# Four sums of weight blocks per pair of gate and up units, formed by accumulating SBUF-to-SBUF transfers from GpSimd instead of by VectorE

## The chip, the cores and the metric

The kernel runs on 1 core of one Trainium2 chip. The metric is the device time of one execution in microseconds (us). Before the change it is 2313.14 us, the median of 3 runs (2313.03 to 2313.42).

## The reference

Two layers of an encoder, for 64 + 512 tokens (columns) of width 1024 that share all weights. Each layer has a feed-forward network (FFN), a mixer and a second FFN, so the kernel runs four FFNs in all:

```
x = x + 0.5 * rmsnorm(swiglu(rmsnorm(x)))      # FFN 1
x = x + rmsnorm(mix(rmsnorm(x)) @ w_out)       # mixer: attention, recurrence, chunk MLP
x = x + 0.5 * rmsnorm(swiglu(rmsnorm(x)))      # FFN 2

def _swiglu(x, w_gate, w_up, w_down):
    return (jax.nn.silu(x @ w_gate) * (x @ w_up)) @ w_down
```

w_gate and w_up are 1024 x 2816, that is 8 x 22 blocks of 128 x 128, in fp32. Only their products with x are touched here.

## The kernel before

A product in fp32 is made of three products of halves: `split` writes a high part (ScalarE, line 138) and the rest, the low part (VectorE, line 139), and `three` issues high*high, high*low and low*high on TensorE (line 68). A weight block of 128 x 1024 (512 KB: four 128-row blocks of gate, four of up) so costs one load (two DMA issues of 256 KB on SP, line 454), one ScalarE pass into a tile wh and one VectorE pass into a tile wl.

The first two of the 22 units of each FFN are multiplied plainly (tiles u). The other twenty go in ten pairs f, f+1 through `seven`, which saves one product in eight: the eight products of a 2 x 2 scheme (two halves of the inner dimension, two units; two halves of the 576 columns on the other side) become seven, of sums of weight blocks with sums of activations. `combine` forms the sums of activations once for each FFN (tiles b, th, tl; lines 427 to 442), just before the first pair. The sums of weights are formed for each pair. With a11, a12 the lower and upper half of unit f's rows and a21, a22 those of unit f+1, the parts are

```
p1 = a11                   p5 = s = a21 + a22
p6 = s + a11               p3 = s + a11 + a12
p7 = a21 + a11             p2 = a12         p4 = a22
```

and TensorE takes them in the order p1, p5, p6, p3, p7, p2, p4, with results in X (p1, p6, p7, p4), Q (p5, p3) and R (p2). s grows in place: each step adds one block after the split of the step before. The four sums of a pair stand at lines 478 (s = a21 + a22), 480 (a21 += a11), 488 (s += a11) and 497 (s += a12), all on VectorE.

Raw blocks live in a pool of six buffers (tile names wr, and ws for s), split blocks in seven pairs of buffers, one for each part. A pair holds five raw buffers, so a buffer passes to the next pair when its block has been read for the last time. The order of instructions on each engine is fixed when the program is built, by a scheduler; every engine and every DMA queue then takes its instructions in that order. SP issues all DMAs, GpSimd does a few small operations of the norms (lines 151 and 198) and of the mixer.

Of the kernel before, what the change touches and what calls it, by code (L numbers as in the profile page):

```python
# [8 lines left out]
F32 = mybir.dt.float32  # L9
# [3 lines left out]
ALU = mybir.AluOpType  # L13
AX = mybir.AxisListType

P = 128
# [33 lines left out]
class Net:  # L50
# [396 lines left out]
    def seven(self, f, wg, wu, ops, g, rbc):  # L447
        nc = self.nc

        def load(k0, c):  # L450
            raw = self.wraw.tile([P, 1024], F32, name=self.name("wr"), tag="wr")
            for e, w in enumerate((wg, wu)):
                src = w.rearrange("(k p) f -> p k f", p=P)[:, k0:k0 + 4, c * P:(c + 1) * P]
                nc.sync.dma_start(raw[:, e * 512:(e + 1) * 512].rearrange("p (k n) -> p k n", k=4), src)
            return raw

        def part(raw):
            hi = self.whi.tile([P, 1024], F32R, name=self.name("wh"), tag="wh")
            lo = self.wlo.tile([P, 1024], F32R, name=self.name("wl"), tag="wl")
            self.split(hi, lo, raw)  # L460
            return hi, lo


        def product(w, b, ps, start):
            for e in range(2):
                for k in range(4):
                    c = e * 512 + k * P
                    h = ops[b][k // 2]
                    s = slice((k % 2) * W2, (k % 2 + 1) * W2)
                    self.three(ps[e][:, :W2], w[0][:, c:c + P], w[1][:, c:c + P], h[0][:, s], h[1][:, s],  # L470
                               start and k == 0, k == 3, not start)
                    self.tick()

        A, B = slice(0, W2), slice(W2, T)
        a11, a21, a22 = load(0, f), load(0, f + 1), load(4, f + 1)
        p1 = part(a11)
        s = self.wraw.tile([P, 1024], F32, name=self.name("ws"), tag="wr")
        nc.vector.tensor_tensor(s, a21, a22, op=ALU.add)
        p5 = part(s)
        nc.vector.tensor_tensor(a21, a21, a11, op=ALU.add)  # L480
        a12 = load(4, f)
        X = [self.mm("X"), self.mm("X")]
        product(p1, "b11", X, True)
        p1 = None
        s1 = [self.slot("s1"), self.slot("s1")]
        for e in range(2):
            nc.scalar.activation(s1[e][:, A], X[e][:, :W2], AF.Copy)
        nc.vector.tensor_tensor(s, s, a11, op=ALU.add)
        a11 = None
        p6 = part(s)  # L490
        Q = [self.mm("Q"), self.mm("Q")]
        product(p5, "t1", Q, True)
        p5 = None
        s5 = self.slot("s5")
        for e, h in enumerate((A, B)):
            nc.scalar.activation(s5[:, h], Q[e][:, :W2], AF.Copy)
        nc.vector.tensor_tensor(s, s, a12, op=ALU.add)  # L497
        p3 = part(s)
        s = None
        product(p6, "t2", X, False)  # L500
        p6 = None
        for e in range(2):
            nc.scalar.activation(s1[e][:, B], X[e][:, :W2], AF.Copy)
        p7 = part(a21)
        a21 = None
        product(p3, "b22", Q, False)
        p3 = None
        g[f] = self.slot("g")
        t = [g[f], s1[1]]
        for e in range(2):  # L510
            nc.vector.tensor_tensor(t[e][:, B], s1[e][:, B], Q[e][:, :W2], op=ALU.add)
        Q = None
        p2 = part(a12)
        a12 = None
        product(p7, "t3", X, False)
        p7 = None
        for e, h in enumerate((A, B)):
            nc.vector.tensor_tensor(s5[:, h], s5[:, h], X[e][:, :W2], op=ALU.add)
        g[f + 1] = self.slot("g")
        nc.vector.scalar_tensor_tensor(g[f + 1][:, B], s5[:, A], -1.0, rbc[:, B], op0=ALU.mult, op1=ALU.mult)  # L520
        p4 = part(a22)
        a22 = None
        R = [self.mm("R"), self.mm("R")]
        product(p2, "b21", R, True)
        p2 = None
        for e in range(2):
            nc.vector.tensor_tensor(t[e][:, A], s1[e][:, A], R[e][:, :W2], op=ALU.add)
        R = None
        nc.vector.tensor_tensor(t[0], t[0], rbc, op=ALU.mult)
        nc.scalar.activation(t[0], t[0], AF.Silu)  # L530
        nc.vector.tensor_tensor(g[f], t[0], t[1], op=ALU.mult)
        s1 = t = None
        product(p4, "t4", X, False)
        p4 = None
        u = g[f + 1]
        nc.vector.scalar_tensor_tensor(u[:, A], X[0][:, :W2], -1.0, rbc[:, A], op0=ALU.mult, op1=ALU.mult)
        nc.scalar.activation(u, u, AF.Silu)
        nc.vector.scalar_tensor_tensor(u[:, B], s5[:, B], -1.0, u[:, B], op0=ALU.mult, op1=ALU.mult)
        nc.vector.scalar_tensor_tensor(u[:, A], X[1][:, :W2], -1.0, u[:, A], op0=ALU.mult, op1=ALU.mult)
# [917 lines left out]
```

## Time and profile before

| | |
|---|---|
| median of 3 runs | 2313.14 us |
| the profiled execution | 2313.43 us, of which the span is 2311.6 us |
| TensorE (PE) busy | 2217.3 us, 96% |
| VectorE (DVE) busy | 1594.7 us, 69% |
| ScalarE (ACT) busy | 1114.0 us, 48% |
| GpSimd (POOL) busy | 225.4 us, 10% |
| DMA queue of SP | 208.54 MB, 30.3% of 16 engines |
| the ten pairs of the first FFN | 60.07 to 278.67 us of the span |

Busy time is summed over the span. The chain of waits follows the work that ended last back from the end, at each step to what released it. PEclk is the granted share of TensorE's clock. The pairs of the four FFNs take some 220 us each; the rest of an FFN is its first two units, the sums of activations and the down projection.

### The profile page before, as it was taken

What the parts mean: (1) busy time and instruction counts of PE and PEld (TensorE: products, weight loads), DVE (VectorE), ACT (ScalarE), POOL (GpSimd) and SP (SyncE); (2) the same over time, 40 slices, a digit from 0 to 9 for tenths busy, and PEclk for the clock granted to TensorE, in tenths of its full rate; (3) what the DMA queues carried; (4) which work ended last, traced back from release to release, by engine and by line L of the source; (5) the groups of instructions that cost most, each with busy time, mean ns of one, the idle gap of its engine ahead of it and who ended that gap; (6) DMA issues with size and microseconds to landing.
All of it is one profiled execution on the core that took longest, in us unless ns stands there. A gap on an engine that the chain in (4) does not pass through costs nothing.

```text
span 2311.6 us, 39493 instructions
## 1 busy us (share of the span) xinstructions
PE 2217.3 (96%) x15892; PEld 2155.0 (93%) x15892; DVE 1594.7 (69%) x2671; ACT 1114.0 (48%) x1945; POOL 225.4 (10%) x230
## 2 busy tenths in 40 slices
PE   8999999998899899999989999999988998999998
PEld 7999999888799799999979999998887998999998
DVE  6888643787567888744588885438875678877443
ACT  7444442465554644443355444325646546444423
POOL 0000000343301100000020000004332020000000
PEclk9999999999999899999999999999999999999999
DMA  6333442222122233344123334423121312333421
GB/s 195 103 101 92 119 133 83 92 57 77 60 59 65 90 101 96 88 128 132 47 86 101 93 90 122 132 74 101 39 86 48 96 60 83 93 92 103 118 77 42
DMA packets 339787, 211.06 MB, mean 91 GB/s; under 512 B 17634, under 2 KB 319956, under 8 KB 339604
## 3 DMA queue, kind: packets, MB, share of 16 engines
q1 hardware_dynamic: 339604, 208.54, 30.3%
q8 instruction: 125, 2.05, 0.4%
q14 instruction: 58, 0.48, 0.1%
HBM read 190.11 MB, written 18.38 MB: 90 GB/s over the span
## 4 chain that ended last, share of the span: by engine, by line
PE 76%; DVE 14%; ACT 4%; issue 3%; POOL 3%; DMA 0%; SPq 0%; POOLq 0%; DVEq 0%; ACTq 0%
PE d L68 23%; PE X L68 22%; PE Q L68 11%; PE R L68 6%; PE wo L68 4%; PE u L68 3%; DVE zb L706 2%; PE n L68 2%; DVE hl L142 2%; DVE x L256 1%; PE sc L68 1%; DVE d L253 1%; DVE wl L127 1%; DVE wl L139 1%; PE q L68 1%
## 5 line engine op out<-in xcount | busy, mean ns | idle before, releaser
L68 PE MATMUL d<-gh,wh 128*128 128x288 f32 x1408 | 413.5, 297 | 2.7 <-ACT gh L138 2.7
L68 PE MATMUL d<-gl,wh 128*128 128x288 f32 x1408 | 413.9, 295 | 0.0
L68 PE MATMUL d<-gh,wl 128*128 128x288 f32 x1408 | 412.7, 294 | 0.0
L127 DVE TENSOR_TENSOR wl<-wr,wh 128x1024 fp32r<-128x1024 f32 (+2 forms) x174 | 203.4, 1173 | 175.9 <-ACT wh L126 175.1
L126 ACT ACTIVATE wh<-wr 128x1024 fp32r<-128x1024 f32 (+2 forms) x174 | 174.8, 1008 | 287.3 <-PE d L68 163.9
L68 PE MATMUL X<-th,wh 128*128 128x288 f32 x960 | 286.8, 299 | 0.0
L68 PE MATMUL X<-tl,wh 128*128 128x288 f32 x960 | 285.5, 297 | 0.0
L68 PE MATMUL X<-th,wl 128*128 128x288 f32 x960 | 284.5, 296 | 0.0
L68 PEld LDWEIGHTS d<-gh,wh 128*128 128x128 f32 x1408 | 262.3, 187 | 3.6 <-ACT gh L138 3.6
L68 PEld LDWEIGHTS d<-gh,wl 128*128 128x128 f32 x1408 | 264.8, 188 | 0.0
L68 PEld LDWEIGHTS d<-gl,wh 128*128 128x128 f32 x1408 | 264.1, 188 | 0.0
L138 ACT ACTIVATE wh<-wr 128x1024 fp32r<-128x1024 f32 x160 | 168.4, 1055 | 148.0 <-PE R L68 68.5
L139 DVE TENSOR_TENSOR wl<-ws,wh 128x1024 fp32r<-128x1024 f32 x120 | 147.0, 1225 | 105.4 <-ACT wh L138 105.2
L139 DVE TENSOR_TENSOR wl<-wr,wh 128x1024 fp32r<-128x1024 f32 x160 | 194.7, 1222 | 8.2 <-ACT wh L138 6.8
L138 ACT ACTIVATE wh<-ws 128x1024 fp32r<-128x1024 f32 x120 | 127.3, 1060 | 150.4 <-DVE ws L497 97.8
L151 POOL TENSOR_TENSOR p<-m,mhalf 128x3 f32<-128x3 f32 (+1 forms) x14 | 14.4, 1028 | 1739.4 <-DVE m L234 1535.1
L68 PEld LDWEIGHTS X<-th,wl 128*128 128x128 f32 x960 | 183.1, 191 | 0.0
L68 PEld LDWEIGHTS X<-tl,wh 128*128 128x128 f32 x960 | 182.8, 190 | 0.0
L68 PEld LDWEIGHTS X<-th,wh 128*128 128x128 f32 x960 | 182.6, 190 | 0.0
L390 DVE TENSOR_TENSOR d<-d,d 128x288 f32<-128x288 f32 x128 | 55.2, 454 | 179.6 <-PE d L68 179.5
L68 PE MATMUL u<-hh,wh 128*128 128x288 f32 x480 | 148.3, 312 | 3.0 <-ACT x L1363 1.5
L68 PE MATMUL u<-hl,wh 128*128 128x288 f32 x480 | 148.0, 309 | 1.2 <-DVE hl L142 1.2
(364 smaller groups left out, 5857.6 us busy)
## 6 DMA issues: line engine op xcount, KB each, us to landing
wr<-ffn_w_gate SPq DMA_DIRECT2D x160, 256.0 KB, 3.0
wr<-ffn_w_up SPq DMA_DIRECT2D x160, 256.0 KB, 3.4
wr<-ffn_w_down SPq DMA_DIRECT2D x64, 512.0 KB, 4.2
wr<-w_in SPq DMA_DIRECT2D x30, 512.0 KB, 3.7
xd<-x SPq DMA_DIRECT2D x48, 288.0 KB, 2.1
x<-xd SPq DMA_DIRECT2D x48, 288.0 KB, 6.0
wr<-ffn_w_down SPq DMA_DIRECT2D x32, 384.0 KB, 3.6
wr<-w_out SPq DMA_DIRECT2D x16, 512.0 KB, 3.4
```

Of the source, the lines that this page charges most:

```text
L68: self.nc.tensor.matmul(out, lhsT, rhs, start=start, stop=stop, skip_group_check=onto)
L126: nc.scalar.activation(hi[:, :a * b], raw[:, :a * b], AF.Copy)
L127: nc.vector.tensor_tensor(lo[:, :a * b], raw[:, :a * b], hi[:, :a * b].bitcast(F32), op=ALU.subtract)
L138: nc.scalar.activation(hi, src, AF.Copy)
L139: nc.vector.tensor_tensor(lo, src, hi.bitcast(F32), op=ALU.subtract)
L142: nc.vector.scalar_tensor_tensor(lo, src, scale, hi.bitcast(F32), op0=ALU.mult, op1=ALU.subtract)
L151: self.nc.gpsimd.tensor_tensor(out, m, self.mhalf[:, :n], op=ALU.pow)
L253: nc.vector.scalar_tensor_tensor(d[s][:, sl], d[s][:, sl], gpost[s], bc, op0=ALU.mult, op1=ALU.mult)
L256: nc.vector.tensor_tensor(self.x[k][:, sl], self.x[k][:, sl], d[k][:, sl], op=ALU.add)
L390: nc.vector.tensor_tensor(d[m][:, sl], d[m][:, sl], ps[hf][:, :n], op=ALU.add)
L706: nc.vector.tensor_tensor(zo, qv[rs, :, h:], ev[rs, :, h:], op=ALU.mult)
```

## The change

s is loaded as a copy of a21 and the four sums are DMAs that GpSimd issues, with addition at the destination. A pair has five loads instead of four (a21 comes twice), in the order s, a22, a11, a21, then a12.

```
-        a11, a21, a22 = load(0, f), load(0, f + 1), load(4, f + 1)
+
+        def onto(dst, src):
+            nc.gpsimd.dma_start(dst, src, accum_op=ALU.add)
+
+        s, a22, a11, a21 = load(0, f + 1), load(4, f + 1), load(0, f), load(0, f + 1)
+        onto(s, a22)
         p1 = part(a11)
-        s = self.wraw.tile([P, 1024], F32, name=self.name("ws"), tag="wr")
-        nc.vector.tensor_tensor(s, a21, a22, op=ALU.add)
+        onto(a21, a11)
+        a12 = load(4, f)
         p5 = part(s)
-        nc.vector.tensor_tensor(a21, a21, a11, op=ALU.add)
-        a12 = load(4, f)
...
-        nc.vector.tensor_tensor(s, s, a11, op=ALU.add)
+        onto(s, a11)
         a11 = None
         p6 = part(s)
...
-        nc.vector.tensor_tensor(s, s, a12, op=ALU.add)
+        onto(s, a12)
         p3 = part(s)
```

The sums now stand at line 477. On GpSimd's queue nothing stood between the norm's last operations of the first FFN's start and the norm after that FFN. Before, at this place (rn, p: factors of a norm; acc: a sum of squares):

```order
L151 ISA
L151 TENSOR_TENSOR rn_130<-m_256,mhalf 128x3
L151 TENSOR_TENSOR rn_130<-m_344,mhalf 128x3
L151 TENSOR_TENSOR p_4475<-m_4472,mhalf 128x3
L198 TENSOR_TENSOR acc_4460<-acc_4460,sq_4536 128x288
L198 TENSOR_TENSOR acc_4460<-acc_4460,sq_4557 128x288
```

With the change, forty transfers stand there, of which these are the first. In the first pair wr_630 is s, wr_633 a22, wr_636 a11, wr_639 a21, wr_648 a12; in the second wr_876, 879, 882, 885 in the same way.

```order
L151 TENSOR_TENSOR rn_130<-m_344,mhalf 128x3
L477 DMA wr_630<-wr_633 128x1024
L477 DMA wr_639<-wr_636 128x1024
L477 DMA wr_630<-wr_636 128x1024
L477 DMA wr_876<-wr_879 128x1024
L477 DMA wr_630<-wr_648 128x1024
L477 DMA wr_885<-wr_882 128x1024
L477 DMA wr_876<-wr_882 128x1024
```

In the queue the second pair's first sum precedes the first pair's last one, and in each pair a21 += a11 precedes s += a11.

On SP's queue a pair from the middle of the first FFN had eight issues, wr_1362, 1365, 1368 and 1382 being a11, a21, a22 and a12:

```order
L454 DMA wr_1362<-ffn_w_gate 128x4x128
L454 DMA wr_1362<-ffn_w_up 128x4x128
L454 DMA wr_1365<-ffn_w_gate 128x4x128
L454 DMA wr_1365<-ffn_w_up 128x4x128
L454 DMA wr_1368<-ffn_w_gate 128x4x128
L454 DMA wr_1368<-ffn_w_up 128x4x128
L454 DMA wr_1382<-ffn_w_gate 128x4x128
L454 DMA wr_1382<-ffn_w_up 128x4x128
```

Now it has ten, here with the semaphores that each waits for (DMAHW: transfers of SP; DMASW: transfers of GpSimd, whose eight semaphores take turns; DMASW1, 2 and 3 are a21 += a11, s += a11 and s += a12 of the pair before). wr_1368, 1371, 1374, 1377 and 1386 are s, a22, a11, a21 and a12:

```order
L454 DMA wr_1368<-ffn_w_up 128x4x128 [waits DMAHW3_49]
L454 DMA wr_1371<-ffn_w_gate 128x4x128 [waits DMAHW4_49,DMASW2_49,DMAHW5_49,DMASW1_49,DVE_49]
L454 DMA wr_1371<-ffn_w_up 128x4x128
L454 DMA wr_1374<-ffn_w_gate 128x4x128 [waits DMAHW6_49,DMASW3_49,DVE_49]
L454 DMA wr_1374<-ffn_w_up 128x4x128 [waits DMAHW7_49]
L454 DMA wr_1377<-ffn_w_gate 128x4x128 [waits DMAHW0_49,DVE_49]
L454 DMA wr_1377<-ffn_w_up 128x4x128 [waits DMAHW1_49]
L454 DMA wr_1386<-ffn_w_gate 128x4x128 [waits DMAHW2_49,DVE_49]
L454 DMA wr_1386<-ffn_w_up 128x4x128 [waits DMAHW3_49]
```

So a22 takes the buffer that the a11 of the pair before left, a11 that of s, a21 that of a21, a12 that of a12, each after the last sum or split that read it.

On TensorE, in the first pair of the first FFN, five products of p2 (R, weights wh_779 and wl_780) stood ahead of the product of p6 (X, weights wh_684):

```order
L68 MATMUL R_815<-hh_168,wh_779 128x288
L68 MATMUL R_815<-hl_169,wh_779 128x288
L68 MATMUL R_816<-hh_168,wh_779 128x288
L68 MATMUL R_816<-hl_169,wh_779 128x288
L68 MATMUL R_815<-hh_168,wl_780 128x288
L68 MATMUL X_653<-th_570,wh_684 128x288
L68 MATMUL X_653<-tl_571,wh_684 128x288
```

Now the product of p6 follows that of p5 (Q) at once. In the other three FFNs thirteen, eight and thirteen products of p2 stand ahead of p6, where five stood before.

```order
L68 MATMUL Q_691<-tl_598,wh_651 128x288
L68 MATMUL Q_691<-th_597,wl_652 128x288
L68 MATMUL X_655<-th_570,wh_686 128x288
L68 MATMUL X_655<-tl_571,wh_686 128x288
L68 MATMUL X_655<-th_570,wl_687 128x288
```

## Rows read from the trace of the kernel before

**Rows 1.** The page, busy times by engine.
```profile
PE 2217.3 (96%) x15892; PEld 2155.0 (93%) x15892; DVE 1594.7 (69%) x2671; ACT 1114.0 (48%) x1945; POOL 225.4 (10%) x230
```
**Rows 2.** Windows: busy us of each engine in stretches, granted clock, DMA share.
```profile
core 0: us, PE busy (x) PEld busy (x) DVE busy (x) ACT busy (x) POOL busy (x), PEclk, DMA share, GB/s
60.07:278.67 218.60, 218.60 (x1630) 218.60 (x1631) 177.97 (x229) 106.07 (x151) 0.00 (x0) 0.99 0.35 102
104.40:126.80 22.40, 22.40 (x171) 22.40 (x170) 18.29 (x24) 10.81 (x16) 0.00 (x0) 1.00 0.33 96
50.00:60.00 10.00, 4.62 (x29) 3.69 (x27) 8.76 (x13) 9.98 (x18) 0.00 (x0) 0.98 0.18 52
780.00:790.00 10.00, 4.43 (x17) 3.50 (x18) 10.00 (x14) 9.75 (x17) 0.00 (x0) 0.66 0.18 52
...
337.00:338.00 1.00, 1.00 (x10) 1.00 (x9) 0.65 (x2) 0.94 (x1) 0.00 (x0) 1.00 1.04 402
```
**Rows 3.** Chain of waits, first FFN: start us, us, what.
```profile
44.16 1.14 DVE wl L139
...
53.93 1.14 DVE wl L139
...
60.07 0.61 PE R L68
...
64.94 3.20 PE Q L68 x24
```
**Rows 4.** Chain of waits, start of the second FFN.
```profile
780.07 0.76 DVE b L436
780.83 0.90 DVE ws L497
781.72 0.15 issue
781.87 0.75 DVE tl L139
782.63 0.37 DVE g L341
782.99 0.67 DVE b L438
...
789.80 0.61 PE R L68
...
795.00 3.20 PE Q L68 x24
```
**Rows 5.** Groups of instructions: busy us, mean ns of one, idle before.
```profile
L139 DVE TENSOR_TENSOR wl<-ws,wh 128x1024 fp32r<-128x1024 f32 x120 | 147.0, 1225 | 105.4 <-ACT wh L138 105.2 <-PE xt L73 0.2
...
L138 ACT ACTIVATE wh<-ws 128x1024 fp32r<-128x1024 f32 x120 | 127.3, 1060 | 150.4 <-DVE ws L497 97.8 <-PE Q L68 35.7 <-DVE ws L488 8.6
...
L478 DVE TENSOR_TENSOR ws<-wr,wr 128x1024 f32<-128x1024 f32 x40 | 49.0, 1225 | 11.8 <-DMA wr<-ffn_w_up 6.2 <-issue 5.6
...
L151 POOL TENSOR_TENSOR p<-m,mhalf 128x3 f32<-128x3 f32 (+1 forms) x14 | 14.4, 1028 | 1739.4 <-DVE m L234 1535.1 <-DVE m L236 198.7 <-DVE m L951 5.7
```
**Rows 6.** DMA issues: count, KB each, median us from issue to landing.
```profile
wr<-ffn_w_up SPq DMA_DIRECT2D x160, 256.0 KB, 3.4
...
xd<-x SPq DMA_DIRECT2D x48, 288.0 KB, 2.1
x<-xd SPq DMA_DIRECT2D x48, 288.0 KB, 6.0
...
st<-state_hgrn SPq DMA_DIRECT2D x8, 16.0 KB, 1.9
...
out_hgrn_p<-st SPq DMA_DIRECT2D x8, 16.0 KB, 1.7
```
**Rows 7.** Timeline of SP's queue within one pair: start us, us.
```profile
109.48 0.37 SPq L454 DMA_DIRECT2D wr<-ffn_w_gate  x1
```

## The prediction

> **What bounds the kernel now.** The page comes first: TensorE is busy 2217.3 us, 96% of the span, VectorE 69% and GpSimd 10% [rows 1]. Then the windows by stage. In the whole stretch of pairs of the first FFN TensorE is busy 218.60 us of 218.60; in one pair of it (104.4 to 126.8) TensorE has 22.40 us of 22.40, VectorE 18.29, ScalarE 10.81, GpSimd nothing, and the DMA engines are at a share of 0.33 [rows 2]. The chain of waits in order of time says the same: from 60.07 us on it holds only TensorE pieces, 3.20 us for a product, 7 x 3.20 = 22.4 us for a pair [rows 3]. So the four sums, 4 x 1.22 = 4.9 us of VectorE per pair [rows 5], stand beside a full TensorE. Their removal is worth nothing there.
>
> The starts of the four FFNs are another matter. In the last 10 us before the pairs run freely TensorE is busy only 4.62 us in the first FFN and 4.43 us in the second [rows 2], and the chain goes through VectorE piece by piece until the split of p2 lets the first five R matmuls go, at 60.07 and 789.80 us [rows 3, 4]; the other two FFNs start as the second does. There, over 5 us four times, a lighter VectorE could pay.
>
> **The change part by part.** *Removed:* 160 adds of 1.22 us, 195 us of VectorE [rows 5]. On the chain of the second FFN's start stands one of them, 0.90 us [rows 4]. In the first FFN's start none does, but there the order of TensorE changes: the five R matmuls no longer stand ahead of the product of p6, so that p2 is not waited for so early.
>
> *Added:* 40 more loads of a block (a21 comes twice) and 160 accumulating transfers of 512 KB. GpSimd is idle in the pairs [rows 2]; what counts is how long a sum is under way.
>
> *Price of one sum.* No row of this trace shows a transfer issued by GpSimd, or an accumulating one. I call L its time from issue to landing, L = fixed + descriptors + X. Fixed: the 16 KB transfers of the state land 1.7 to 1.9 us after issue [rows 6]; I take 1.8. Descriptors, what GpSimd itself needs to issue one: nothing, or as long as its smallest operation, 1.03 us [rows 5]; I take 1.0, since even 128 x 3 elements cost this engine that much. X, the transfer: the DMA engines move 402 GB/s at a share of 1.04 [rows 2], so 512 KB take 1.3 us as a copy. An accumulation reads two operands and writes one: 1.3 us if all three overlap, 2.6 us if the two reads follow each other, 3.9 us if nothing overlaps. I take 2.6, the middle, because a copy already overlaps its one read and its one write. So L = 5.4 us, with 3.1 (1.8 + 0 + 1.3) and 6.7 us (1.8 + 1.0 + 3.9) as the ends. The same sum on VectorE took 1.22 us.
>
> *What waits for it.* In a pair, s takes a22, is split (p5), takes a11, is split (p6), takes a12, is split (p3): three sums in a row, with splits between, since a sum may not overwrite what a split still reads. And there is a ring from pair to pair, through the six raw buffers and the in-order queues of SP and GpSimd. The a11 of a pair loads into the buffer that s of the pair before leaves when p3 is split, its a21 into the one that p7 leaves; GpSimd's queue has a21 += a11 ahead of s += a11, so the latter waits for that load too, whatever state s is in. Once round:
>
> - p3 split, then p7 split: 1.2 us on VectorE [rows 5];
> - load of a21: the issue of its first half takes SP 0.4 us [rows 7], the second is issued then and lands 3.4 us later [rows 6]: 3.8 us;
> - a21 += a11 with s += a11 behind it in the same queue: L + X;
> - p6 split, 1.06 on ScalarE and 1.22 on VectorE [rows 5]: 2.3 us; then s += a12: L; then p3 split: 2.3 us.
>
> Together 9.6 + 2L + X, which is 23.0 us with my values. To that comes what the loads take from the sums on the same DMA engines. Four blocks cost 0.33 x 22.4 = 7.4 us of all engines per pair [rows 2], 1.85 us a block; of the five loads I count one, that of the next s, which is issued with the load of a12 and so runs beside a21 += a11. That such neighbours slow each other the trace shows: eight recalls of x in a row, behind loads, land after 6.0 us, while 288 KB of x stored land after 2.1 us [rows 6]. The Trainium skill has it as a rule that speaks against this change ("DMA: Bandwidth & Descriptors", section "Issuing engines are not separate DMA queues"): transfers of SP and of GpSimd run on the same 16 engines and interleave. Without the term the ring takes 23.0 us and the sum below becomes 2323 us, with it 24.85 us. That is 2.45 us over TensorE's 22.4.
>
> *First FFN.* The split of p5 ends at 45.3 us (44.16 + 1.14) [rows 3]; s += a11 lands L later, 50.7. Only then is a11's buffer free for a22 of the second pair, which lands 3.8 us later, 54.5. In GpSimd's queue this pair's first sum stands ahead of s += a12 of the first pair, so the latter lands L + X later, at 62.5, and p3 is split at 64.8 (45.3 + L + 3.8 + L + X + 2.3). Before, its product began at 64.94 [rows 3]: a gain of 0.2 us at the start. Nine pairs follow, each 2.45 us longer: 22.0 - 0.2 = 21.8 us.
>
> *Second to fourth FFN.* Here R stays ahead of p6's product, and TensorE starts when p2 is split. VectorE's chain loses the add (0.90 us), but p3's split, which stands ahead of p2's, now waits for a transfer: p6 split until 780.07, then L, then 1.06 on ScalarE, 786.5. VectorE would come to it at 780.07 + 0.76 + 0.15 + 0.75 + 0.37 + 3 x 0.67 = 784.1 [rows 4] (the order puts two more b operations ahead of it); so it comes L - 2.9 = 2.5 us late, and the start moves by 2.5 - 0.9 = 1.6 us. The ring has room at first: p3 is split at 786.5 + 1.2 = 787.7 and wanted at 795.00 + 1.6 = 796.6, 8.9 us later. Nine pairs take 22.0 us, 13.1 more than that room. Each of these FFNs pays 1.6 + 13.1 = 14.7 us, three of them 44.1.
>
> *Sum.* 21.8 + 44.1 = 65.9 us on the profiled execution's 2313.43 us (a span of 2311.6 with 1.8 us around it; the median of the three runs is 0.3 us below): 2379.3, say **2379 us**. Downs and mixers keep their order on TensorE, and no sum runs in them but the first of the next FFN, which has time.
>
> With the low end, L = 3.1 and X = 1.3, the ring takes 9.6 + 6.2 + 1.3 + 1.85 = 19 us and hides behind TensorE. Then only the starts count. In the first, s += a12 still waits for p6's split, which ends at about 54.5 (in the place of the split that began at 53.93 [rows 3]): 54.5 + 3.1 + 2.3 = 59.9 in place of 64.94, 5.0 us less. In the others 0.2 late less 0.9: 0.7 us less each. Sum 7.1: 2306 us. With the high end, L = 6.7 and X = 3.9, the ring takes 28.75 us: first FFN 3.7 + 9 x 6.35 = 60.9, the others 2.9 + 57.2 - 8.9 = 51.2 each: 2528 us.
>
> **The rivals.**
> 1. *Faster* (the other side): a sum costs hardly more than a copy, the ring stays under 22.4 us, and TensorE starts earlier in each FFN: 2306 us. For it: GpSimd and two thirds of the DMA time are free [rows 2]. Against: it needs L below 3.8 us, as with 1.0 us of descriptors and X = 1.3 it is 4.1 and the sum is only -4.0 + 3 x 0.3 = -3.1 us. From the point where 9.6 + 1.85 + 2L + X passes 22.4, the other side decides. A price for a GpSimd transfer stands in the Trainium skill ("DMA: Bandwidth & Descriptors", section "Anatomy of one DMA", the GpSimd path): 2.0 us plus the bytes at 436 GB/s, by which I would estimate L = 3.2 us for 512 KB and a time near 2307 us. [...]
> 2. *No change*: L between 3.8 and 4.6 us; the starts give a little or nothing, the ring is hidden. 2313 us, give or take 4.6 (0.2%, about what a measurement of this kernel can tell from no change).
> 3. *Far slower*: three passes that don't overlap, 2528 us. For it: 512 KB read twice and written once are 1.5 MB through engines that move 0.4 MB in 1 us [rows 2]. Against: a copy's read and write overlap.
> That the sums stay on VectorE is excluded by the order.
>
> **How the numbers follow.** Forecast (ring longer than TensorE's pair by 0.3 to 5 us) 0.50; far slower 0.16; no change 0.17; faster 0.17. So faster 0.17, same 0.17, slower 0.66. The range goes from the low end, 2305, to the high end, 2530, and leaves out perhaps 0.15, nearly all above. The slower cases' own range is 2320 to 2530.
>
> **What would show it.** In the new profile: 160 transfers of 512 KB issued by GpSimd at L477, landing after about 5.4 us alone and later in pairs; VectorE near 13.4 us per pair; gaps of TensorE once per pair, ahead of the product of p3 or of p6, released through ScalarE's or VectorE's split by a GpSimd transfer, absent in the first three pairs of the second to fourth FFN and in each later pair of 2 to 3 us; pairs of about 24.9 us in the chain. If pairs remain at 22.4 us, my L or the ring is wrong, and only the starts can differ. If the gaps are there from the first pair and much longer, X is. Wrong in kind would be a wait on GpSimd's own queue that I don't see: descriptors that take several us each, or norm operations of GpSimd behind a waiting sum at the start of an FFN.

## The result, and the profile after

The changed kernel takes **2441.38 us**, the median of 4 runs (2435.97 to 2444.61), against 2313.09 us for the kernel before, run beside it: a ratio of 1.0554, with an interval of 1.0534 to 1.0575. It is 128 us slower; the prediction was 2379 us. The profiled execution has a span of 2440.3 us, 128.7 us more than before.

The page, first the busy times by engine, then what the queues moved:

```profile
PE 2256.7 (92%) x15892; PEld 2176.2 (89%) x15892; DVE 1410.9 (58%) x2511; ACT 1092.0 (45%) x1945; POOL 362.8 (15%) x390
...
q1 hardware_dynamic: 381844, 229.52, 32.0%
q0 software_dynamic: 23040, 83.90, 18.2%
```

VectorE is busy 184 us less than in [rows 1], and nothing is gained by it; TensorE falls from 96% to 92%. 83.90 MB in 160 sums is 0.52 MB each, and 18.2% of the span is 444 us of all 16 DMA engines, 2.78 us for one sum.

The windows of nine pairs of the first and of the second FFN, one pair of the second, and a stretch of the first:

```profile
core 0: us, PE busy (x) PEld busy (x) DVE busy (x) ACT busy (x) POOL busy (x), PEclk, DMA share, GB/s
66.30:302.80 236.50, 212.69 (x1513) 207.69 (x1514) 128.15 (x177) 95.57 (x141) 30.73 (x35) 0.97 0.78 182
834.50:1064.30 229.80, 208.71 (x1502) 203.53 (x1501) 121.38 (x171) 90.59 (x135) 28.57 (x33) 0.99 0.76 178
...
850.30:875.10 24.80, 22.92 (x170) 22.45 (x169) 12.15 (x18) 9.31 (x15) 3.46 (x4) 1.00 0.83 192
...
108.80:115.60 6.80, 6.11 (x25) 6.11 (x26) 3.60 (x8) 2.12 (x3) 1.77 (x2) 0.50 0.89 187
```

Before, TensorE filled every stretch of pairs and the DMA share was 0.33 [rows 2]. Now nine pairs take 236.5 and 229.8 us, in which TensorE stands idle for 23.8 and 21.1 us. The share of 0.83 says that the DMA engines are busier, not that they are the bound; experiments decide that below. The last row is one of the stretches in which TensorE, after it had waited, was granted 1.2 GHz only.

The DMA issues, with the median from issue to landing last:

```profile
wr<-wr POOLq DMA_DIRECT2D x160, 512.0 KB, 5.7
wr<-ffn_w_gate SPq DMA_DIRECT2D x200, 256.0 KB, 3.7
wr<-ffn_w_up SPq DMA_DIRECT2D x200, 256.0 KB, 4.1
```

The group of GpSimd's issues (busy us, mean ns of one, idle before and its releasers):

```profile
L477 POOL DMA_DIRECT2D wr<-wr x160 | 139.9, 877 | 1161.2 <-DVE wl L139 314.1 <-DVE s L521 302.9 <-DMA wr<-ffn_w_up 276.6
```

A sum lands 5.7 us after its issue, 4.5 us at the least; GpSimd needs 0.88 us to issue it; loads land 0.7 us later than in [rows 6]. The releasers say what GpSimd's queue waits for: splits and loads. The profile infers a releaser from the time at which it ends. Where it names an evacuation (L521), the sum needs only the split just ahead of it in VectorE's queue: s += a12 may not overwrite s before p6's split has read it.

The chain of waits through the pair of the second FFN from 850.3 to 875.1 us, with the split of p3 ahead of it:

```profile
848.03 1.07 ACT wh L138
...
851.92 4.90 DMA wr<-ffn_w_up
...
857.50 0.85 POOL wr L477
858.35 0.68 issue
859.05 6.34 DMA wr<-wr
...
865.47 1.07 ACT wh L138
...
866.56 1.23 DVE wl L139
867.79 0.38 DVE s L521
...
868.19 4.55 DMA wr<-wr
...
872.85 1.07 ACT wh L138
```

There is no TensorE in it. p3 is split (848.03), a21's load lands, a21 += a11 is issued, then s += a11 (6.34 us, with a21 += a11 still under way), p6 is split, s += a12 (4.55 us), p3 is split again (872.85), and the next load can go: from one split of p3 to the next 24.8 us, once round the ring of the prediction. Where TensorE feels it is in its list of waits (us in total, times, longest):

```profile
PE X L68 <- DVE s L521: 44.4, 31, 3.1
PE X L68 <- ACT s L490: 37.1, 34, 3.5
```

TensorE hardly ever waits for the split weights themselves. It waits for evacuations of X: L521 on VectorE must have read X after p7 before the product of p4 may write there, and L490 on ScalarE after p1 before that of p6. Both stand in in-order queues behind splits that wait for transfers. The order of VectorE's queue shows it (wr_1614 is s of the next pair, so wl_1671 belongs to its p6; X_1393 and X_1394 belong to this pair):

```
132 L139 TENSOR_TENSOR wl_1671<-wr_1614,wh_1670 128x1024
133 L521 TENSOR_TENSOR s_211_1454<-s_211_1454,X_1393 128x288
134 L523 SCALAR_TENSOR_TENSOR g_1549<-s_211_1454,rbc_129 128x288
135 L521 TENSOR_TENSOR s_211_1454<-s_211_1454,X_1394 128x288
```

### The profile page after: what moved, and what is told of

Its sections match the earlier page's. It is cut to its first block, busy times and chain, and to the rows that moved or that the text cites. A ratio compares the mean times of both kernels' runs of the same rounds, so it can differ in the third digit from the quotient of the medians.

```text
span 2440.3 us, 40159 instructions
## 1 busy us (share of the span) xinstructions
PE 2256.7 (92%) x15892; PEld 2176.2 (89%) x15892; DVE 1410.9 (58%) x2511; ACT 1092.0 (45%) x1945; POOL 362.8 (15%) x390
## 3 DMA queue, kind: packets, MB, share of 16 engines
q0 software_dynamic: 23040, 83.90, 18.2%
## 4 chain that ended last, share of the span: by engine, by line
PE 41%; DMA 24%; DVE 16%; issue 8%; ACT 6%; POOL 4%; SPq 1%; POOLq 0%; DVEq 0%; ACTq 0%
PE d L68 22%; DMA wr<-wr 17%; DMA wr<-ffn_w_up 6%; PE wo L68 4%; DVE wl L139 3%; PE X L68 3%; PE u L68 3%; ACT wh L138 3%; DVE zb L709 2%; DVE hl L142 1%; PE sc L68 1%; DVE x L256 1%; POOL wr L477 1%; DVE d L253 1%; PE Q L68 1%
## 5 line engine op out<-in xcount | busy, mean ns | idle before, releaser
L139 DVE TENSOR_TENSOR wl<-wr,wh 128x1024 fp32r<-128x1024 f32 x280 | 338.4, 1224 | 359.8 <-ACT wh L138 358.4
L138 ACT ACTIVATE wh<-wr 128x1024 fp32r<-128x1024 f32 x280 | 287.4, 1053 | 541.5 <-DMA wr<-wr 489.7
L68 PE MATMUL X<-th,wh 128*128 128x288 f32 x960 | 300.2, 313 | 81.6 <-DVE s L521 44.4
L477 POOL DMA_DIRECT2D wr<-wr x160 | 139.9, 877 | 1161.2 <-DVE wl L139 314.1
L68 PE MATMUL X<-tl,wh 128*128 128x288 f32 x960 | 291.5, 304 | 0.0
L68 PE MATMUL X<-th,wl 128*128 128x288 f32 x960 | 290.2, 302 | 0.0
L68 PEld LDWEIGHTS X<-th,wl 128*128 128x128 f32 x960 | 188.5, 196 | 0.0
L68 PEld LDWEIGHTS X<-tl,wh 128*128 128x128 f32 x960 | 188.2, 196 | 0.0
L68 PE MATMUL u<-hh,wl 128*128 128x288 f32 x480 | 148.9, 311 | 0.0
L68 PE MATMUL Q<-th,wh 128*128 128x288 f32 x320 | 96.3, 303 | 12.2 <-ACT th L138 8.0
```

What stands on the lines that cost most here:

```text
L68: self.nc.tensor.matmul(out, lhsT, rhs, start=start, stop=stop, skip_group_check=onto)
L138: nc.scalar.activation(hi, src, AF.Copy)
L139: nc.vector.tensor_tensor(lo, src, hi.bitcast(F32), op=ALU.subtract)
L477: nc.gpsimd.dma_start(dst, src, accum_op=ALU.add)
```

## The experiments

Times of p3's product from one pair to the next are read from the trace (start of its first matmul; the second FFN, nine steps); before, they are 21.7 and then 22.4 throughout. The main ones in one table:

```
changed kernel        21.9 26.6 25.2 26.1 26.3 25.7 26.6 26.4 24.8
plain copies          20.7 22.4 22.4 22.4 22.4 22.4 22.4 22.4 22.4
sums on VectorE       21.3 22.4 22.4 22.4 22.4 22.4 22.4 22.4 22.4
8 buffers             22.8 30.5 26.6 26.7 26.6 27.3 29.2 25.3 23.1
8, order kept         21.2 23.8 24.0 23.2 24.1 25.8 22.6 24.1 23.3
8, and L521 ahead     21.2 22.5 24.0 24.0 24.2 23.6 22.8 23.8 22.4
6, and L521 ahead     20.7 28.5 22.6 26.1 24.1 24.6 26.6 24.1 24.3
sums on GpSimd        21.6 22.8 23.9 24.1 23.9 23.9 23.9 23.9 23.9
a21 += a11 alone      21.7 22.4 22.4 22.4 22.4 22.4 22.4 22.4 22.4
```

### Plain copies in place of sums

```diff
-            nc.gpsimd.dma_start(dst, src, accum_op=ALU.add)
+            nc.gpsimd.dma_start(dst, src)
```

> Leaves out the additions: the 160 transfers by GpSimd stay where they are, with the same operands, buffers and order, but as plain copies. The ring theory (a round of loads, splits and transfers through the six raw buffers and the in-order queues sets the 25.7 us of a pair): one transfer takes about 1.4 us of all DMA engines in place of the 2.77 us seen in the changed kernel, three of them stand in the round, so the round falls to 25.7 - 3 x 1.4 = 21.5 us, under TensorE's 22.4: 2310 to 2330 us. Rival 'it is that transfers are issued by GpSimd at all, or the fifth load and the new order': the round keeps its length, 2430 us or more.

Measured: 2313.92 us, ratio 1.0004 (0.9994 to 1.0013). GpSimd's queue and its issues in the view of the DMAs:

```profile
q0 software_dynamic: 23040, 83.90, 9.2%
...
wr<-wr POOLq DMA_DIRECT2D x160, 512.0 KB, 3.5
```

The window of one pair of its second FFN:

```profile
834.60:857.00 22.40, 22.40 (x170) 22.40 (x169) 14.58 (x22) 10.83 (x18) 2.13 (x4) 1.00 0.68 220
```

The same packets and bytes, half the time of the engines, and 3.5 us to landing in place of 5.7. GpSimd's own time for an issue falls too, from 0.88 to 0.53 us (2.13 us for four). That GpSimd issues transfers, the fifth load and the order cost next to nothing; the accumulation's own duration is what it takes to make the ring longer than TensorE's pair. The run halves the work of the DMA engines together with the time to landing, and does not tell the two apart; the runs with eight buffers do.

### Sums on VectorE with the changed kernel's loads

```diff
-            nc.gpsimd.dma_start(dst, src, accum_op=ALU.add)
+            nc.vector.tensor_tensor(dst, dst, src, op=ALU.add)
```

> The loads, their order and the fifth load of the changed kernel, but the four sums by VectorE on the same operands. The ring theory (the transfers' own latency is the cause): a sum takes 1.22 us, the round has some 12 us less, 2308 to 2320 us. Rival 'the fifth load of each pair and the order that s and a22 come ahead of a11 are the cause': 2400 us or more.

Measured: 2315.91 us, ratio 1.0019 (1.0010 to 1.0028). The fifth load and the new order cost some 4 us, and its pairs run at 22.4 us. The rest is the transfers.

### One sum alone as a transfer

```diff
-        nc.vector.tensor_tensor(a21, a21, a11, op=ALU.add)
+        nc.gpsimd.dma_start(a21, a11, accum_op=ALU.add)
```

> The kernel before with one of its four sums alone as an accumulating transfer by GpSimd: a21 += a11, which only the split of p7 reads; the three sums into s stay on VectorE, with the loads of before. Theory: a sum costs by where it stands; this one is in no round that is longer than TensorE's pair (load of a21, sum 4.6 to 6.3 us, p7 split, about 14 us), so 2308 to 2317 us, as before. Rival 'each accumulating transfer takes its share of the DMA engines and so costs its quarter': 2345 us, or 2330 at least.

Measured: 2312.98 us, ratio 1.0004 (0.9995 to 1.0013). Its issues:

```profile
wr<-wr POOLq DMA_DIRECT2D x40, 512.0 KB, 5.5
```

The window of one pair:

```profile
834.60:857.00 22.40, 22.40 (x170) 22.40 (x170) 17.15 (x22) 10.68 (x15) 0.85 (x1) 1.00 0.49 118
```

The transfer is as slow as in the changed kernel, and TensorE does not notice. This sum, for which no next step of the ring waits, costs nothing; no quarter of the loss goes with a quarter of the transfers.

### Eight raw buffers, and the control

```diff
-                tc.tile_pool(name="wraw", bufs=6) as net.wraw, \
+                tc.tile_pool(name="wraw", bufs=8) as net.wraw, \
...
-                tc.tile_pool(name="slots", bufs=57) as net.slots, \
+                tc.tile_pool(name="slots", bufs=55) as net.slots, \
```

> Eight raw buffers in place of six (and 55 slots in place of 57, to have the room), sums as in the changed kernel. The ring theory: a11, a21 and a12 of a pair no longer load into what the splits of p3 and p7 of the pair before give back last, so the round is broken; pairs of 22.4 to 22.8 us once they run, with only the starts of the four FFNs still dearer: 2315 to 2335 us. Rival 'the DMA engines are full' (share 0.83 in a pair of 24.8 us, so it would have to be 0.92 in one of 22.4): pairs stay at 25 us, 2425 us or more.

> Control for the run with eight raw buffers: six of them, and 55 slots alone. Both theories: as the changed kernel, 2441 us, give or take 8.

Measured: 2478.67 us (1.0711, 1.0693 to 1.0729) with eight buffers, and 2443.35 us (1.0567, 1.0551 to 1.0582) for the control. Slower than the changed kernel, so the expectation failed, and yet the rival's reason need not hold. GpSimd's queue shows what else moved (wr_1368 and wr_1377 are s and a21 of one pair, wr_1614 is s of the next):

```
28 L477 DMA wr_1377<-wr_1374 128x1024
29 L477 DMA wr_1614<-wr_1617 128x1024
30 L477 DMA wr_1368<-wr_1374 128x1024
31 L477 DMA wr_1368<-wr_1386 128x1024
```

With room for it, the first sum of the next pair has been put ahead of two sums of this one. TensorE's waits for L521 rise from 44.4 to 85.5 us, by its list of waits:

```profile
PE X L68 <- DVE s L521: 85.5, 30, 5.5
```

### Eight buffers, the sums of a pair kept together

```diff
-            nc.gpsimd.dma_start(dst, src, accum_op=ALU.add)
+            with self.behind(self.lastsum): self.lastsum = nc.gpsimd.dma_start(dst, src, accum_op=ALU.add)
```

(behind queues an instruction after the one given, on its engine.)

> Eight raw buffers and 55 slots as in the run that took 2479 us, with each sum kept behind the one traced before it in GpSimd's queue, so that the four sums of a pair stay together. Theory: the eight buffers failed because the first sum of the next pair had moved ahead of s += a11 of this one in GpSimd's in-order queue, and so waited for loads into buffers that this pair gives back late; with the order of the changed kernel and the two more buffers the round is broken: 2315 to 2345 us. Rival 'more buffers only bring more loads beside the sums, and the engines are full': 2440 us or more.

Measured: 2372.17 us (1.0263, 1.0246 to 1.0280). That is 106.5 us less than without it, by the order of one queue, and 69 us less than the changed kernel: the buffers do shorten the ring that the prediction drew, and GpSimd's queue order had hidden it. The rival, that more loads beside the sums must lose, is wrong. But pairs stayed near 24 us, and the expected 2315 to 2345 was missed: another round remained.

### Also the evacuations ahead of the next pair's split

```diff
-        p6 = part(s)
+        with self.behind(self.last521): p6 = part(s)
...
-            nc.vector.tensor_tensor(s5[:, h], s5[:, h], X[e][:, :W2], op=ALU.add)
+            self.last521 = nc.vector.tensor_tensor(s5[:, h], s5[:, h], X[e][:, :W2], op=ALU.add)
```

On eight buffers with the sums kept together:

> The kernel with eight raw buffers and the sums of a pair kept together (2372 us), and on VectorE the evacuations of X after p7 kept ahead of the low split of p6 of the next pair. Theory: what was left there, pairs of 24 us, is a round through TensorE: p6 split, then the evacuation that stands behind it on VectorE, the products of p4 and p1 (6.4 us), ScalarE's evacuation of X after p1 with the splits of p1 and p5 behind it, s += a11 (5.3), p6 split. With the evacuation ahead, the round is open: pairs of 22.4 to 22.6 us, 2312 to 2335 us. Rival 'transfers beside loads are slowed, and that is the 24 us': 2360 us or more.

Measured: 2359.06 us (1.0210, 1.0194 to 1.0225), 13 us less, and not the 37 us or more that I expected. The window of one pair of it:

```profile
880.00:904.00 24.00, 22.64 (x170) 22.41 (x170) 13.74 (x20) 9.90 (x16) 3.49 (x4) 1.00 0.90 198
```

ScalarE's timeline from p3's split to p5's of the next pair:

```profile
874.25 1.06 ACT L138 ACTIVATE wh<-wr 128x1024 fp32r<-128x1024 f32 x1 [3.25 <-DMA wr<-wr]
875.21 0.67 ACT L545 ACTIVATE g<-g 128x576 f32<-128x576 f32 x1
875.79 1.99 ACT L138 ACTIVATE wh<-wr 128x1024 fp32r<-128x1024 f32 x2
877.68 0.39 ACT L495 ACTIVATE s<-X 128x288 f32<-128x288 f32 x1
877.97 1.05 ACT L138 ACTIVATE wh<-wr 128x1024 fp32r<-128x1024 f32 x1
...
880.45 1.07 ACT L138 ACTIVATE wh<-wr 128x1024 fp32r<-128x1024 f32 x1
```

p5's split (880.45), which needs only the first sum, stands last in ScalarE's queue behind everything from p3's split (874.25) on; then come s += a11, which here lands 7.35 us after its issue, p6's split, s += a12 and p3's split again, 24 us later. The round is now closed by ScalarE's order. The edit moved more than it names: on VectorE p3's low split now stands behind the pair before's reading of X after p4, and on ScalarE the pair before's last Silu (L545) right behind p3's split, where it stood behind p4's. The round's length grows with the transfers beside it: at a share of 0.90 the median sum lands after 6.6 us.

On six buffers, with the sums in the changed kernel's order (but for the second pair's first sum, which in each FFN now stands behind the first pair's last):

> Six raw buffers as in the changed kernel, the sums kept in its order in GpSimd's queue, and the evacuations of X after p7 ahead of the low split of p6 of the next pair. Theory: the ring of transfers stays (load of a11 4.6, splits of p1 and p5 3.7, s += a11 6.3, p6 split 2.8, s += a12 4.6, p3 split 2.4: 24.4 to 25 us), but TensorE feels it only when the weights themselves are late, so the room of about 8.9 us returns in the second to fourth FFN, and pairs of 25.2 to 26.6 come down to 24.8: 2385 to 2415 us. Rival 'the ring alone counts': 2430 to 2445 us.

Measured: 2411.60 us (1.0434, 1.0419 to 1.0450), 30 us less than the changed kernel and within the expectation. In the nine steps of the second to fourth FFN it is 18 us, where the theory had 27. So the order of the queues does cost time that the prediction's room was to save; as VectorE's and ScalarE's queues changed in other places too, as in the run before, not all of it need be the one evacuation's. And the room did not come back as three pairs of 22.4 us: the second pair takes 28.5 us (24.5 and 29.0 in the third and fourth FFN). The waits for VectorE's evacuation are gone from TensorE's list, and those for ScalarE's have risen from 37.1 us (L495 is L490 of the changed kernel, and still behind p3's split), as its list of TensorE's waits has it:

```profile
PE X L68 <- ACT s L495: 58.5, 31, 4.1
```

The 28.5 us are one such wait and the clock. s += a12 lands at 865.97 us, ScalarE then splits p3, p7 and p2 and comes to L495 at 869.51, and TensorE has stood idle for 3.3 us. After that it is granted 1.2 GHz for 6.8 us: in the window from 847.3 to 875.8 us the granted clock is 0.88 on average and TensorE is busy for 25.2 us in place of 22.4.

### ScalarE's evacuation ahead too

```diff
-        p2 = part(a12)
+        with self.behind(l490): p2 = part(a12)
...
-        p4 = part(a22)
+        with self.behind(l490): p4 = part(a22)
```

With the edit to p6 above, on six buffers, and without keeping the sums together (l490 is the second evacuation of X after p1).

> The sums as in the changed kernel; on VectorE the second evacuation of X after p7 is kept ahead of the low split of p6 of the next pair, and on ScalarE the evacuations of X after p1 ahead of the splits of p2 and p4 of the same pair. Theory: the prediction's room of 8.9 us at the start of the second to fourth FFN was lost because evacuations stand in the in-order queues behind splits that wait for a transfer, so that TensorE feels the lateness some 9 us before the weights are wanted; with them ahead the room is back, 3 x 8.9 = 27 us less, and the pairs in the steady state stay at 25.7: 2405 to 2425 us. Rival 'the ring alone counts, wherever the evacuations stand': 2436 to 2446 us.

Measured: 2534.78 us (1.0969, 1.0953 to 1.0986), the slowest of all, so it tells nothing clean of the room. TensorE's waits for the very evacuation that was moved (L495) rose from 37.1 to 173.3 us. In GpSimd's queue the next pair's first sum had moved ahead of s += a12 of this pair, and GpSimd's waits for a load rose from 276.6 to 508.4 us, by GpSimd's list of waits:

```profile
POOL wr L482 <- DMA wr<-ffn_w_up: 508.4, 47, 25.8
```

### The order of a21 += a11, and of p5's split

```diff
-        onto(a21, a11)
...
-        onto(s, a11)
+        with self.behind(onto(s, a11)): onto(a21, a11)
```

> The same four transfers, loads and buffers as the changed kernel, but in GpSimd's queue a21 += a11 stands behind s += a11, in place of ahead of it. The ring theory: s += a11 then neither waits for the load of a21 nor shares the engines with a sum queued just ahead; the round becomes p3 split 1.2, load of a11 into the buffer of s 3.8, s += a11 5.7, p6 split 2.3, s += a12 with a sum ahead of it 7, p3 split 1.1 on ScalarE = 21 us, under 22.4: 2315 to 2350 us. Rival 'the DMA engines' work sets the pair' (the same bytes): no change, 2430 us or more.

Measured: 2477.07 us (1.0714, 1.0698 to 1.0730), worse, where I expected 2315 to 2350. The chain of waits, one round:

```profile
176.09 4.93 DMA wr<-ffn_w_up
...
181.09 4.29 issue
...
185.39 4.58 DMA wr<-wr
...
190.06 1.07 ACT wh L138
...
191.15 1.23 DVE wl L139
...
192.78 6.34 DMA wr<-wr
```

s += a11 takes 4.58 us now, but s += a12 takes 6.34 in place of 4.55, beside the two halves of a load that SP issues at 192.67 and 193.08 us (a21 += a11 had landed at 192.55). Between the load's landing and the sum lie 4.29 us: the load is a11's, and s += a11 waits for p5's split, which stands behind p1's, which waits for that load. So p5's split goes first:

```diff
-        p1 = part(a11)
...
+        with self.behind(self.hl[0]), self.behind(self.hl[1]): p1 = part(a11)
```

(hl holds the two passes of the split traced last, here p5's.)

> As the run with a21 += a11 behind s += a11 (2477 us), and the split of p5 ahead of that of p1 on ScalarE and VectorE. Theory: there s += a11 did not come earlier because it waits for the split of p5, which stands in ScalarE's queue behind that of p1, which waits for the load of a11 (the 4.3 us between the load's landing and the sum in the chain of waits). With p5 split first, s += a11 follows the load by 0.6 us, 3.4 us less per pair than 27: pairs of 22.5 to 24 us, 2320 to 2380 us. Rival 'the sums slow each other, whatever their order': 2440 us or more.

Measured: 2425.81 us (1.0492, 1.0475 to 1.0510). 51 us less than without the edit, so that wait was real; but 2320 to 2380 was not reached. The queues had been drawn anew around the edit, and TensorE waited again for evacuations on ScalarE, one of them (L508, after p6) behind the p6 split of the next pair. Its list of waits:

```profile
PE X L68 <- ACT s L508: 39.4, 29, 3.1
PE X L68 <- ACT s L492: 35.0, 30, 5.7
```

### The sums on GpSimd, without transfers

```diff
-        nc.vector.tensor_tensor(s, s, a11, op=ALU.add)
+        nc.gpsimd.tensor_tensor(s, s, a11, op=ALU.add)
```

(all four sums of the kernel before so)

> The kernel before, with its four sums computed by GpSimd on SBUF in place of VectorE, no transfer and no fifth load. Estimated from GpSimd's 128x288 (0.98 us) and 128x576 (1.58 us) operations, a 128x1024 sum takes 2.5 us, 10 us per pair. Theory: the time of the sum decides and not the engine; 2.5 us fits in the room, VectorE has 4.9 us less per pair off the path: 2305 to 2318 us. Rival 'sums off VectorE cost the pair whoever makes them, by the hand-over between engines': over 2330 us.

Measured: 2390.81 us (1.0340, 1.0325 to 1.0355), where I expected no change. Pairs settle at 23.9 us with a DMA share of 0.31, and no engine is full:

```profile
856.00:879.90 23.90, 22.81 (x169) 22.44 (x169) 17.35 (x20) 10.68 (x16) 11.01 (x4) 1.00 0.31 89
```

In its timeline, two VectorE operations and two GpSimd sums beside each other:

```profile
885.24 3.26 DVE L139 TENSOR_TENSOR wl<-wr,wh 128x1024 fp32r<-128x1024 f32 x1
888.42 2.66 DVE L538 SCALAR_TENSOR_TENSOR g<-s,g 128x288 f32<-128x288 f32 x1
...
885.01 2.41 POOL L478 TENSOR_TENSOR ws<-wr,wr 128x1024 f32<-128x1024 f32 x1 [8.09 <-DVE g L531]
887.50 3.27 POOL L480 TENSOR_TENSOR wr<-wr,wr 128x1024 f32<-128x1024 f32 x1
```

With sums of 2.4 us and more in place of 1.22 a round closes: it goes load, two sums, p5's split, sum, p6's split, sum, p3's split, load. And the two engines delay each other: a low split of 1.22 us takes 3.26 while GpSimd's sum runs. The Trainium skill has it ("SBUF — State Buffer", section "Who interferes with whom"): an instruction of VectorE with two SBUF inputs and one of GpSimd that reads SBUF hold a shared port in turn. The trace agrees: the sum that began at 885.01 us ends at 887.42, and the split that began at 885.24 ends 1.1 us later. How much of the 1.5 us per pair is the sums' own time and how much the delay was not separated.

## Why the prediction was right in sign and too small

*That VectorE's 4.9 us per pair are worth nothing:* right. Taking one off (a21 += a11) left 2313 us.

*Price of one sum:* nearly right. I had X = 2.6 us and it is 2.78; 1.0 us for GpSimd's issue and it is 0.88; L = 5.4 and it is 4.5 at the least and 5.7 in the median, as others share the engines. 4.5 less 2.78 and 0.88 leaves 0.8 us for the fixed part, where I had 1.8. L + X, from the issue of a21 += a11 to the landing of s += a11 behind it, was 8.0 and is 7.9 in the chain above (857.50 to 865.39), of which 0.7 is a wait for p5's split. The rule of the Trainium skill that the prediction cited against the change ("DMA: Bandwidth & Descriptors", section "Issuing engines are not separate DMA queues") holds here: loads land 0.7 us later beside the sums (4.1 us in the median, 4.2 beside plain copies, 3.5 with the same loads and no transfers). The estimate of 3.2 us by the Trainium skill ("DMA: Bandwidth & Descriptors", section "Anatomy of one DMA") lies near the copies' 3.5 us; for an accumulation the measured 4.5 us and more decides.

*The ring:* right in kind. 24.85 us was predicted and the round in the chain above has 24.8. That they agree so closely is in part luck: the load's second half took 4.90 us in place of 3.4, s += a12 4.55 in place of 5.4, and the 1.85 us put down for a neighbour are not found as a piece of their own. The round has two branches that end within 0.7 us of each other: through a21's load and a21 += a11, as predicted, and through a11's load and the splits of p1 and p5, which here ends last (the 0.68 us "issue" ahead of s += a11 at 859.05 is how much later). I had the first alone; the run with a21 += a11 behind lost the first and so gained nothing. Since the rounds also cross TensorE through evacuations, the mean from the second step on, in the second to fourth FFN, is 25.7 us.

*The room of 8.9 us in the second to fourth FFN:* **this step failed.** It took the weights as wanted at p3's product. Earlier, TensorE wants X and Q evacuated, and those evacuations stand behind the late splits in the queues of VectorE and ScalarE. So the lateness shows from the second step on (26.6 us in the table), not from the fourth. In the second to fourth FFN the pairs cost 28.8, 25.5 and 27.5 us against 13.1 predicted each: 42.5 us more, of which 3 x 8.9 = 26.7 are the room, and the rest the longer round. The two lists of waits show the evacuations, and the run with L521 ahead on six buffers takes 18 us less in these stretches.

*The starts:* -0.2 and 1.6 us each were predicted; p3's first product is late by 1.5 us in the first FFN and by a further 2.7, 1.1 and 6.1 us in the others. That is 11.5 in place of 4.6 us. Over half of the 6.1 us is there when that FFN's first units start, behind a mixer in which no sum runs; where it comes from stays open.

*The first FFN's pairs:* 22.0 us predicted, 35.5 measured. Its first two steps took 29.0 and 28.3 us.

*The sum:* starts 11.5, pairs 117.2 (35.5 and, rounded, 81.8): 128.7 us, of which 65.9 were predicted. A second account of the 117.2 us in the pairs: by windows of the nine steps of each FFN, TensorE was idle for 83 us and busy for 34 us longer than before, 11.7 us of it in the first FFN (212.69 less 201.00). Part of that is the clock, of which the prediction said nothing. After waits of 1.9 to 3.5 us, nine in all, it was granted 1.2 GHz for 13.7, 6.8, 3.4 and 10.2 us of the four stretches, before never. In the 6.8 us shown above 25 matmuls took 6.11 us, 0.24 us each, against 22.40 / 171 = 0.13 in [rows 2]; so 34 us at the lower level, some 140 matmuls, cost at most 16 us. The other 18 us of longer busy time are not explained here (the ends of matmuls are modelled in the profile).

*The rivals:* three passes that don't overlap (X = 3.9) fell by X = 2.78, and with it 2528 us. Full DMA engines were mine only as a share of 1.85 us; that they are not the bound is shown by the pairs of 24 us at a share of 0.90, against 24.8 at 0.83, and by a pair of the same run on eight buffers (1255.0 to 1277.4 us) in which TensorE is busy for all of its 22.40 us at a share of 0.93. What a fuller set of engines does is to let each sum land later, and so to lengthen a round.

**What stays open:** how much of the lost room each of the two evacuations holds, as no run moved one of them alone. A kernel with each of the four sums as transfers and pairs of 22.4 us throughout was not found. None of the versions beat the kernel before.

## What to carry to other kernels

To offload an operation from an engine that is not the bound, price its latency, not its busy time: 1.22 us of VectorE became 4.5 to 6.5 us until the result is there, twice in one dependent round with a third sum queued ahead, and the round passed TensorE's pair. In in-order queues a late operand delays all that stands behind it, so ask of each waiting split which evacuation or issue follows it, and when that one is wanted. Every edit of such a kernel redraws several queues: compare the order of all of them before a run is read.

## What the runs showed of the hardware

- An accumulating SBUF-to-SBUF transfer of 512 KB takes 2.78 us of all 16 DMA engines, twice a copy's (18.2% of the span against 9.2%), and lands 4.5 us after issue at the least, a copy after 2.8 us. GpSimd's issue of one took 0.88 us, of a copy 0.53 us.
- A GpSimd sum of two 128x1024 operands in SBUF takes 2.4 us alone and up to 3.3 beside VectorE, and stretches VectorE's split from 1.22 to 3.26 us.
- Nine waits of TensorE of 1.9 to 3.5 us in the four stretches of pairs were each followed by a stretch at 1.2 GHz: 34 us in all.
